# Moving the start of the large SBUF pools to multiples of 2048 bytes in a two-layer pool and SSD trunk

## The chip, the cores and the metric

The kernel runs on one core of one Trainium2 chip. The metric is the time of one execution on the device in microseconds (us); less is better. One further execution was profiled, and all rows below come from that one.

## The reference, cut to what matters

Two layers of the same form run one after the other on 256 tokens of 2048 channels, all in float32:

```python
h = rms_norm(x, pre_norm_w[layer])
proj = jnp.einsum('bld,de->ble', h, w_in[layer])      # 2048 -> 9248 columns
y_pool = pool_mixer(pool_u, pool_mix_w[layer], pool_scale[layer]) * silu(pool_gate)
y_ssd = ssd_branch(ssd_z, ssd_xbc, ssd_dt, ...)       # conv, chunked scan, gated norm
mixed = concatenate([y_pool, y_ssd])                  # 4096 channels
out = jnp.einsum('ble,ed->bld', mixed, w_out[layer])
x = x + rms_norm(out, post_norm_w[layer])
```

`pool_mixer` takes a trailing mean over 2, 4, 8 or 16 tokens, subtracts the token itself, and multiplies each of four channel groups with a 512 x 512 matrix.

## The kernel before, in words

Each float32 value that goes into a large product is split into a rounded high part and a rest, both of type float32r: `hs` holds the normalised input, `ms` and `pm` the two halves of `mixed`, `pl` the pooled channels, each as [128 partitions, k, 512] where the first 256 of the 512 columns are the high parts of the 256 tokens and the other 256 the rests. The weights come through a stream of 1 MB pieces: the SP queue loads a piece into one of three `raw` buffers (L122), ScalarE rounds half a piece to `wh` (L138), VectorE subtracts to get `wl` (L139), with five `wh` and five `wl` buffers.

In the input projection, and in the pool's 512 x 512 product, the weights are stationary and the activations move. `mm_m` (L330) issues a pair of matmuls for each 128 x 128 block of weights: L334 moves all 512 columns past `wh`, L336 moves the 256 high columns past `wl`. There are 2304 such pairs with `hs` (16 of them from `mm_k`, L342 and L344) and 128 with `pl`. In the output projection `out_mm` (L734) holds a block of `ms` or `pm` stationary and moves 512 columns of weights past it, three matmuls at a time (L741 to L743), 1536 in all. Every one of these matmuls loads its own stationary block.

Between the pairs PE gets the small products of the SSD branch, in plain float32: transposes (L288, L503), dt columns (L677), scores (L491), the scan's products (L537, L542), sums over channels (L325, L562). They are emitted by generators (`ssd`, `dt_chain`) that advance by one step at each `step_bg()` of `chunk`, so that their place among the large matmuls is set by the order of the program. Priorities (`P_SPLIT`, `P_EVAC`, `P_DT`) order the work on the other engines.

Where a tile lies in SBUF is set by the order in which the pools are opened and by the sizes in them. Each pool starts where the one opened ahead of it ends, and the first starts at byte 16512 of each partition. Before the change the order is `const`, `big`, `wts`, `work`. `const` takes 5120 bytes, so `big` starts at byte 21632, which is 1152 past a multiple of 2048. All tiles of `big` (`hs` and `pm` in one place, `ms`, `s16`) and of `wts` (`raw`, `wh`, `wl`) are multiples of 2048 bytes long, so all of them start at 1152 past a multiple of 2048. A [128, 512] float32 slice is 2048 bytes in each partition, a [128, 128] block of weights 512. In `work` lie the 4352-byte `t4` tiles, the 2048-byte `t2`, the 1024-byte `t1`, small tiles, and two buffers of 8192 bytes with the tag `t8`, which hold in turn the dt weights, `BC` (the scan's B and C), the broadcast decay, `pl` and the post-norm weights `pwb`. The `t8` buffers start at bytes 202432 and 210624, 1728 past a multiple of 2048.

The lines that the change and the prediction touch are the pools (L47 to L50), `t8` (L58), the constants (L205 to L233), `pl` (L704), `pwb` (L723) and the matmuls named above.

Of the kernel before, what the change touches and what calls it, by code (L numbers as in the profile page):

```python
# [8 lines left out]
F32 = mybir.dt.float32  # L9
F32R = mybir.dt.float32r  # L10
# [4 lines left out]
P = 128  # L15
D_MODEL = 2048
SEQ = 256
DEPTH = 2
NK = D_MODEL // P
NT = SEQ // P  # L20
CW = 512
# [9 lines left out]
NG = 4  # L31
# [10 lines left out]
def hybrid_kernel(ctx: ExitStack, tc, x, pre_norm_w, w_in, pool_mix_w, pool_scale, conv_w, conv_b,  # L42
# [1 line left out]
    nc = tc.nc  # L44
    PSUM = bass.MemoryType.PSUM

    const = ctx.enter_context(tc.tile_pool(name="const", bufs=1))  # L47
    big = ctx.enter_context(tc.tile_pool(name="big", bufs=1))
    wts = ctx.enter_context(tc.tile_pool(name="wts", bufs=1))
    work = ctx.enter_context(tc.tile_pool(name="work", bufs=1))  # L50
    dram = ctx.enter_context(tc.tile_pool(name="dram", bufs=1, space=bass.MemoryType.DRAM))
    ps_main = ctx.enter_context(tc.tile_pool(name="ps_main", bufs=4, space=PSUM))
    ps_aux = ctx.enter_context(tc.tile_pool(name="ps_aux", bufs=4, space=PSUM))
# [2 lines left out]
        return big.tile([P, 4, NT, CW], F32, name="s16", tag="s16", bufs=1)  # L56

    def t8():  # L58
        return work.tile([P, 8, SEQ], F32, name="t8", tag="t8", bufs=2)

    def t4():
        return work.tile([P, 4, PAD + SEQ], F32, name="t4", tag="t4", bufs=6)
# [116 lines left out]
    def drain_bg():  # L179
        while bg:  # L180
            step_bg()
# [23 lines left out]
    pre_rows = const.tile([DEPTH * NK, P], F32, name="pre_rows")  # L205
    load_pieces(x_in, emit_raw)

    ident = const.tile([P, P], F32, name="ident")
    make_identity(nc, ident)
    ones = const.tile([P, P], F32, name="ones")  # L210
    nc.vector.memset(ones, 1.0)
    upper = const.tile([P, P], F32, name="upper")
    nc.gpsimd.affine_select(out=upper, in_=ones, compare_op=ALU.is_ge, fill=0.0, base=0,
                            pattern=[[1, P]], channel_multiplier=-1)
    after = const.tile([P, P], F32, name="after")
# [3 lines left out]
    nc.vector.memset(eps, EPS)  # L219
    table = const.tile([P, 1], F32, name="table")  # L220
    nc.scalar.activation(out=table, in_=eps, func=AF.Copy)
    fac = const.tile([P, NG, 16], F32, name="fac")
    nc.gpsimd.memset(fac, 1.0)
    for g, w in enumerate(WINDOWS):
        for t in range(w - 1):
# [4 lines left out]
        nc.sync.dma_start(out=raw, in_=w_in[l, :, O_DT:O_DT + NH].rearrange("(k p) c -> p k c", p=P))  # L230
        return raw

    pre_cols = const.tile([P, DEPTH * NK], F32, name="pre_cols")  # L233
    def keep_busy(dst, n, after=None):
        with behind(after):
            for _ in range(n):
                ins = nc.tensor.matmul(dst[:, 0:P], ident, ident, start=True, stop=True, skip_group_check=True)  # L237
        return ins
# [108 lines left out]
    def chunk(mov, nk, pre_unit=None, mid_unit=None, by_k=False):  # L347
        acc = [main() for _ in range(4)]
        nq = nk // 4

        def mid(q, i):
            if mid_unit is not None:
                mid_unit(q, i)
            if q < nq - 1:
                step_bg()

        for q in range(nq):
            if pre_unit is not None:
                pre_unit(q)
            if q == 0 and by_k:  # L360
                hf = [next_half(), next_half()]
                for h in range(2):
                    for kk in range(2):
                        for m in range(4):
                            mm_k(acc, m, hf[h], mov, 2 * h, kk)
                        if h == 1:
                            mid(q, kk)
            elif 0 < q < nq - 1:
                for h in range(2):
                    hf = next_half()  # L370
                    for m in range(4):
                        mm_m(acc, m, hf, mov, 4 * q + 2 * h, False, False)
                    mid(q, h)
            else:
                last = q == nq - 1
                hf = [next_half(), next_half(not last)]
                for m in range(4):
                    for h in range(2):
                        mm_m(acc, m, hf[h], mov, 4 * q + 2 * h, q == 0 and h == 0, last and h == 1)
                    if m % 2 == 1:  # L380
                        mid(q, m // 2)
        return acc
# [8 lines left out]
    def evac(acc, dest, rb, sums=None):  # L391
        for m in range(4):
            t = halves_sum(acc[m]) if sums is None else sums[m]
            nc.gpsimd.tensor_tensor(out=dest[:, m], in0=t, in1=rb, op=ALU.mult)  # L394

    def conv_silu(l, acc, rb, ct0, dst, sums=None):
        pad = t4()
        nc.gpsimd.memset(pad[:, :, 0:KCONV - 1], 0.0)
        evac(acc, pad[:, :, KCONV - 1:KCONV - 1 + SEQ], rb, sums)
        cw = prm[l]["convw"]  # L400
        cb = prm[l]["convb"]
        for m in range(4):
            ct = ct0 + m
            nc.vector.tensor_scalar(out=dst[:, m], in0=pad[:, m, 3:3 + SEQ], scalar1=cw[:, 3, ct:ct + 1],
                                    scalar2=cb[:, ct:ct + 1], op0=ALU.mult, op1=ALU.add)
            for j in (2, 1, 0):
                nc.vector.scalar_tensor_tensor(out=dst[:, m], in0=pad[:, m, j:j + SEQ],  # L407
                                               scalar=cw[:, j, ct:ct + 1], in1=dst[:, m],
                                               op0=ALU.mult, op1=ALU.add)
        nc.scalar.activation(out=dst, in_=dst, func=AF.Silu)  # L410
# [212 lines left out]
    for l in range(DEPTH):  # L623
# [61 lines left out]
        for g in range(NG):  # L685
            acc = chunk(hs, NK)
            if g == 0:
                drain_bg()
            xs = t4()[:, :, 0:SEQ]
            conv_silu(l, acc, rb, 4 * g, xs)  # L690
            res = {}
            bg.append(ssd(l, g, st, xs, BC, res, ms))

            acc = chunk(hs, NK)
            zs = t4()[:, :, 0:SEQ]
            evac(acc, zs, rb)
            nc.scalar.activation(out=zs, in_=zs, func=AF.Silu)
            res["zs"] = zs

            acc = chunk(hs, NK)  # L700
            u = t4()
            nc.gpsimd.memset(u[:, :, 0:PAD], 0.0)
            evac(acc, u[:, :, PAD:PAD + SEQ], rb)
            pl = work.tile([P, 4, CW], F32R, name="pl", tag="t8", bufs=2)  # L704
            pool_window(g, u, pl)

            acc = chunk(hs, NK)
            gs = t4()[:, :, 0:SEQ]
            evac(acc, gs, rb)
            nc.scalar.activation(out=gs, in_=gs, func=AF.Silu)  # L710

            acc = chunk(pl, 4)
            for m in range(4):
                t = halves_sum(acc[m])
                nc.vector.scalar_tensor_tensor(out=pr[:, 4 * g + m], in0=t,
                                               scalar=prm[l]["scale"][:, 4 * g + m:4 * g + m + 1],
                                               in1=gs[:, m], op0=ALU.mult, op1=ALU.mult)
            if g == 1 and l + 1 < DEPTH:
                bg.append(load_params(l + 1))
        drain_bg()  # L720

        load_pieces(x_in if l == 0 else x_mid)
        pwb = work.tile([P, D_MODEL], F32, name="pwb", tag="t8", bufs=2)  # L723
        nc.gpsimd.dma_start(out=pwb, in_=post_norm_w[l].partition_broadcast(P))
        pm = big.tile([P, NK, CW], F32R, name="pm", tag="hs", bufs=1)
        for g in range(NG):
# [129 lines left out]
```

## Time and profile before

| | us |
|---|---|
| median of three runs | 1278.93 |
| lowest and highest | 1278.65, 1279.44 |
| the profiled execution | 1280.09 |
| its span, first to last instruction | 1278.3 |
| PE busy in the span | 1265.3 |

PE is TensorE's matmuls, PEld its weight loads, DVE VectorE, ACT ScalarE, POOL GpSimd, SP the queue that issues most DMAs. Matmuls are pipelined, so that the duration of one is longer than the distance to the next: what a matmul costs in a dense stream is read from the distance of the starts.

### The profile page before, as it was taken

What the parts mean: (1) busy time and instruction counts of PE and PEld (TensorE: products, weight loads), DVE (VectorE), ACT (ScalarE), POOL (GpSimd) and SP (SyncE); (2) the same over time, 40 slices, a digit from 0 to 9 for tenths busy, and PEclk for the clock granted to TensorE, in tenths of its full rate; (3) what the DMA queues carried; (4) which work ended last, traced back from release to release, by engine and by line L of the source; (5) the groups of instructions that cost most, each with busy time, mean ns of one, the idle gap of its engine ahead of it and who ended that gap; (6) DMA issues with size and microseconds to landing.
All of it is one profiled execution on the core that took longest, in us unless ns stands there. A gap on an engine that the chain in (4) does not pass through costs nothing.

```text
span 1278.3 us, 17942 instructions
## 1 busy us (share of the span) xinstructions
PE 1265.3 (99%) x7010; PEld 1084.8 (85%) x7010; DVE 919.0 (72%) x1299; ACT 707.0 (55%) x891; POOL 193.0 (15%) x244
## 2 busy tenths in 40 slices
PE   8999999999999999999999999999999999999997
PEld 7788888888888888888878888888888888888886
DVE  5898778868778794444478988778788788844454
ACT  6656556566566574344374566566565665644442
POOL 0111212212213220000002122122112122200000
PEclk9999999999999999999999999999999999999999
DMA  8555455464464676555564654555654654865552
GB/s 278 201 198 198 165 199 203 152 237 165 165 242 154 207 269 204 190 188 194 188 214 162 220 177 168 203 193 168 227 198 139 223 195 168 296 198 197 192 187 83
DMA packets 126973, 249.49 MB, mean 195 GB/s; under 512 B 9272, under 2 KB 10120, under 8 KB 125608
## 3 DMA queue, kind: packets, MB, share of 16 engines
q1 hardware_dynamic: 124792, 237.25, 54.8%
q0 software_dynamic: 1504, 10.55, 2.2%
q8 instruction: 55, 0.90, 0.3%
q10 hardware_dynamic: 592, 0.54, 0.1%
q14 instruction: 30, 0.25, 0.1%
HBM read 244.06 MB, written 4.26 MB: 194 GB/s over the span
## 4 chain that ended last, share of the span: by engine, by line
PE 99%; DVE 0%; DMA 0%; ACT 0%; issue 0%; ACTq 0%
PE acc L334 44%; PE acc L336 22%; PE acc L743 9%; PE acc L741 9%; PE acc L742 9%; PE aux L537 1%; PE aux L677 1%; PE aux L542 1%; PE aux L288 1%; PE aux L503 1%; DMA pre_rows<-in_pre_norm_w_dram 0%; PE acc L342 0%; DVE t L759 0%; PE aux L562 0%; PE aux L491 0%; PE aux L237 0%
## 5 line engine op out<-in xcount | busy, mean ns | idle before, releaser
L334 PE MATMUL acc<-hs,wh 128*128 128x512 f32 x2288 | 805.4, 396 | 1.0 <-DVE hs L298 1.0
L139 DVE TENSOR_TENSOR wl<-raw,wh 128x1024 fp32r<-128x1024 f32 x431 | 535.5, 1251 | 249.9 <-ACT wh L138 249.9
L138 ACT ACTIVATE wh<-raw 128x1024 fp32r<-128x1024 f32 x431 | 451.2, 1058 | 408.1 <-PE acc L334 215.8
L336 PE MATMUL acc<-hs,wl 128*128 128x256 f32 x2288 | 639.5, 280 | 0.0
L334 PEld LDWEIGHTS acc<-hs,wh 128*128 128x128 f32 x2288 | 428.5, 187 | 101.1 <-issue 1.7
L336 PEld LDWEIGHTS acc<-hs,wl 128*128 128x128 f32 x2288 | 431.8, 189 | 1.1 <-DVE wl L139 0.2
L394 POOL TENSOR_TENSOR t<-t,rb 128x256 f32<-128x256 f32 x144 | 139.5, 977 | 414.9 <-DVE t L388 375.1
L387 ACT COPY t<-acc 128x256 f32<-128x256 f32 x176 | 63.0, 366 | 69.2 <-PE acc L336 69.0
L741 PE MATMUL acc<-wh,pm 128*128 128x512 f32 x256 | 99.7, 389 | 0.0
L742 PE MATMUL acc<-wl,ms 128*128 128x512 f32 x256 | 99.6, 389 | 0.0
L743 PE MATMUL acc<-wh,ms 128*128 128x512 f32 x256 | 99.6, 389 | 0.0
L743 PE MATMUL acc<-wh,pm 128*128 128x512 f32 x256 | 99.6, 389 | 0.0
L742 PE MATMUL acc<-wl,pm 128*128 128x512 f32 x256 | 99.6, 389 | 0.0
L741 PE MATMUL acc<-wh,ms 128*128 128x512 f32 x256 | 99.6, 389 | 0.0
L388 DVE TENSOR_TENSOR t<-acc,t 128x256 f32<-128x256 f32 x176 | 71.3, 416 | 14.4 <-ACT t L387 13.6
L407 DVE SCALAR_TENSOR_TENSOR t<-t,cols,t 128x256 f32<-128x256 f32 x144 | 71.2, 525 | 0.1
L743 PEld LDWEIGHTS acc<-wh,ms 128*128 128x128 f32 x256 | 48.1, 188 | 10.0
L742 PEld LDWEIGHTS acc<-wl,pm 128*128 128x128 f32 x256 | 48.1, 188 | 10.0
L743 PEld LDWEIGHTS acc<-wh,pm 128*128 128x128 f32 x256 | 48.1, 188 | 10.0
L741 PEld LDWEIGHTS acc<-wh,ms 128*128 128x128 f32 x256 | 48.1, 188 | 9.9
L742 PEld LDWEIGHTS acc<-wl,ms 128*128 128x128 f32 x256 | 48.1, 188 | 9.9
L741 PEld LDWEIGHTS acc<-wh,pm 128*128 128x128 f32 x256 | 48.1, 188 | 9.9
(155 smaller groups left out, 841.8 us busy)
## 6 DMA issues: line engine op xcount, KB each, us to landing
raw<-in_w_in_dram SPq DMA_DIRECT2D x143, 1024.0 KB, 4.9
raw<-in_w_out_dram SPq DMA_DIRECT2D x64, 1024.0 KB, 5.1
t<-acs POOLq DMA_DIRECT2D x8, 1024.0 KB, 5.1
raw<-in_pool_mix_w_dram SPq DMA_DIRECT2D x8, 1024.0 KB, 5.1
t<-in_x_dram SPq DMA_DIRECT2D x7, 512.0 KB, 8.9
pwb<-in_post_norm_w_dram POOLq DMA_DIRECT2D x2, 1024.0 KB, 6.5
x_mid<-t SPq DMA_DIRECT2D x8, 256.0 KB, 2.4
t<-x_mid SPq DMA_DIRECT2D x4, 512.0 KB, 7.9
```

What stands on the lines that cost most here:

```text
L138: hi = nc.scalar.activation(out=wh, in_=r, func=AF.Copy)
L139: lo = nc.vector.tensor_tensor(out=wl, in0=r, in1=wh.bitcast(F32), op=ALU.subtract)
L288: ins = nc.tensor.transpose(out=pts[k4 % 2][:, o + T * P:o + (T + 1) * P], in_=xp[c][:, T, k4 * P:(k4 + 1) * P], identity=ident)
L334: nc.tensor.matmul(acc[m], wh[:, kk, cs], mov[:, k0 + kk, :], start=first and kk == 0, stop=False, skip_group_check=True)
L336: stream["mm"] = nc.tensor.matmul(acc[m][:, 0:SEQ], wl[:, kk, cs], mov[:, k0 + kk, 0:SEQ], start=False, stop=last and kk == 1, skip_group_ ...
L387: nc.scalar.copy(out=t[0:n], in_=acc[0:n, SEQ:CW])
L388: nc.vector.tensor_tensor(out=t[0:n], in0=acc[0:n, 0:SEQ], in1=t[0:n], op=ALU.add)
L394: nc.gpsimd.tensor_tensor(out=dest[:, m], in0=t, in1=rb, op=ALU.mult)
L407: nc.vector.scalar_tensor_tensor(out=dst[:, m], in0=pad[:, m, j:j + SEQ], scalar=cw[:, j, ct:ct + 1], in1=dst[:, m], op0=ALU.mult, op1=ALU ...
L741: nc.tensor.matmul(oacc[T], ah, wh[:, kk], start=first and kk == 0, stop=False)
L742: nc.tensor.matmul(oacc[T], ah, wl[:, kk], start=False, stop=False)
L743: nc.tensor.matmul(oacc[T], al, wh[:, kk], start=False, stop=last and kk == 1)
```

## The change

A new pool `first` is opened ahead of the others and takes `ident`, `ones`, `upper` (512 bytes each), `fac` (256) and `pre_cols` (128), 1920 bytes together. With the 16512 bytes in front of it that makes 18432, nine times 2048, and there `big` starts. The rest of the constants stays in `const`, which is now opened last. The two `t8` buffers, and with them `pl` and `pwb`, move from `work` to `wts`. So `hs`, `pm`, `ms`, `s16`, `raw`, `wh`, `wl` and the `t8` buffers start at multiples of 2048, and `work` starts at one. No instruction is added, removed or given another shape.

```diff
-    const = ctx.enter_context(tc.tile_pool(name="const", bufs=1))
+    first = ctx.enter_context(tc.tile_pool(name="first", bufs=1))
     big = ctx.enter_context(tc.tile_pool(name="big", bufs=1))
     wts = ctx.enter_context(tc.tile_pool(name="wts", bufs=1))
     work = ctx.enter_context(tc.tile_pool(name="work", bufs=1))
+    const = ctx.enter_context(tc.tile_pool(name="const", bufs=1))
...
     def t8():
-        return work.tile([P, 8, SEQ], F32, name="t8", tag="t8", bufs=2)
+        return wts.tile([P, 8, SEQ], F32, name="t8", tag="t8", bufs=2)
...
-    ident = const.tile([P, P], F32, name="ident")
+    ident = first.tile([P, P], F32, name="ident")
...
-    ones = const.tile([P, P], F32, name="ones")
+    ones = first.tile([P, P], F32, name="ones")
...
-    upper = const.tile([P, P], F32, name="upper")
+    upper = first.tile([P, P], F32, name="upper")
...
-    fac = const.tile([P, NG, 16], F32, name="fac")
+    fac = first.tile([P, NG, 16], F32, name="fac")
...
-    pre_cols = const.tile([P, DEPTH * NK], F32, name="pre_cols")
+    pre_cols = first.tile([P, DEPTH * NK], F32, name="pre_cols")
...
-            pl = work.tile([P, 4, CW], F32R, name="pl", tag="t8", bufs=2)
+            pl = wts.tile([P, 4, CW], F32R, name="pl", tag="t8", bufs=2)
...
-        pwb = work.tile([P, D_MODEL], F32, name="pwb", tag="t8", bufs=2)
+        pwb = wts.tile([P, D_MODEL], F32, name="pwb", tag="t8", bufs=2)
```

## Rows read from the trace of the kernel before

**Rows 1.** The page, parts 1 and 2: busy time, and clock in 40 slices

```profile
PE 1265.3 (99%) x7010; PEld 1084.8 (85%) x7010; DVE 919.0 (72%) x1299; ACT 707.0 (55%) x891; POOL 193.0 (15%) x244
PEclk9999999999999999999999999999999999999999
```

**Rows 2.** The page, part 4: the chain that ended last, by engine

```profile
PE 99%; DVE 0%; DMA 0%; ACT 0%; issue 0%; ACTq 0%
```

**Rows 3.** Waits of the whole span: waiter, releaser, us in total, times, longest

```profile
ACT wh L138 <- DMA raw<-in_w_out_dram: 2.6, 1, 2.6
PE acc L334 <- DVE hs L298: 1.0, 1, 1.0
```

**Rows 4.** Busy time by stage: us, then each engine's busy time, clock, DMA

```profile
0.00:32.00 32.00, 27.63 (x156) 24.36 (x157) 17.60 (x32) 20.61 (x43) 2.33 (x38) 1.00 0.87 277
630.00:660.00 30.00, 28.97 (x158) 24.09 (x156) 21.12 (x33) 16.75 (x31) 0.11 (x1) 1.00 0.64 201
1268.00:1278.30 10.30, 2.73 (x13) 1.92 (x11) 4.80 (x8) 1.70 (x4) 1.69 (x1) 0.77 0.54 204
```

**Rows 5.** Timeline of PE, output projection of layer 0: start, duration, instruction

```profile
500.49 0.39 PE L741 MATMUL acc<-wh,pm 128*128 128x512 f32 x1
...
505.93 0.39 PE L741 MATMUL acc<-wh,pm 128*128 128x512 f32 x1
```

**Rows 6.** Timeline of PE, 157.5 to 200 us: `hs`, then `pl`, then `hs`

```profile
157.54 0.39 PE L334 MATMUL acc<-hs,wh 128*128 128x512 f32 x1
...
159.27 0.40 PE L334 MATMUL acc<-pl,wh 128*128 128x512 f32 x1
159.50 0.28 PE L336 MATMUL acc<-pl,wl 128*128 128x256 f32 x1
...
164.93 0.39 PE L334 MATMUL acc<-hs,wh 128*128 128x512 f32 x1
165.16 0.28 PE L336 MATMUL acc<-hs,wl 128*128 128x256 f32 x1
165.27 0.40 PE L334 MATMUL acc<-hs,wh 128*128 128x512 f32 x1
...
199.94 0.39 PE L334 MATMUL acc<-hs,wh 128*128 128x512 f32 x1
```

**Rows 7.** Timeline of PE behind L542, 124 to 142 us

```profile
124.24 1.16 PE L542 MATMUL aux<-scs,t 128*128 128x128 f32 x8
...
125.94 0.40 PE L334 MATMUL acc<-hs,wh 128*128 128x512 f32 x1
...
141.84 0.40 PE L334 MATMUL acc<-hs,wh 128*128 128x512 f32 x1
```

**Rows 8.** The chain in order of time: start, us, plain float32 matmuls

```profile
101.46 0.43 PE aux L491 x2
104.89 0.87 PE aux L503 x8
...
201.15 0.43 PE aux L491 x2
```

**Rows 9.** Groups by line and form: count, busy us, mean ns, idle before

```profile
L139 DVE TENSOR_TENSOR wl<-raw,wh 128x1024 fp32r<-128x1024 f32 x431 | 535.5, 1251 | 249.9 <-ACT wh L138 249.9
L759 DVE SCALAR_TENSOR_TENSOR t<-s,r,t 128x512 f32<-128x512 f32 x15 | 11.0, 766 | 0.2
L574 DVE TENSOR_TENSOR pm<-s,pm 128x1024 fp32r<-128x1024 f32 x8 | 10.0, 1270 | 0.0
L574 DVE TENSOR_TENSOR pl<-t,pl 128x1024 fp32r<-128x1024 f32 x8 | 9.6, 1194 | 0.0
```

## Prediction, made before the change was run

> **What bounds the kernel now.** I read the page's busy time first: PE is busy for 1265.3 of 1278.3 us, at the full clock in all 40 slices [rows 1]. Next the chain that ended last: 99% of it is PE [rows 2]. Then the waits: the longest of a weight split for a landing is one of 2.6 us, and PE itself waited 1.0 us for its input [rows 3]. The stages show where PE is idle at all: 32.00 - 27.63 = 4.4 us at the start, 1.0 us between the layers, 7.6 us at the end [rows 4], together the 13.0 us that busy time and span differ by. So the change can pay in one way only: a matmul must follow the one before it sooner. The other engines' durations can touch no more than those 13 us.
>
> Busy time doesn't show the distance of matmuls, so I went to the starts. In the output projection 24 matmuls of 512 columns start between 500.49 and 505.93 us: 5.44 / 24 = 226.7 ns each [rows 5]. In the input projection 100 pairs of 512 + 256 columns start between 165.27 and 199.94 us: 34.67 / 100 = 346.7 ns a pair [rows 6]. With a fixed price a for each matmul and b for a column, a + 512b = 226.7 and 2a + 768b = 346.7 give b = 0.417 ns and a = 13.3 ns. That b is one column a cycle at 2.4 GHz, the level granted, so the columns leave nothing to gain. The a is the question: 2 x 2432 pairs' matmuls and 1536 others are 6400 matmuls, and 6400 x 13.3 = 85 us, the most that any layout could free. The dense stream makes up 2432 x 0.3467 + 1536 x 0.2267 = 1191 us of the span.
>
> **The change part by part.** No instruction and no wait is added, removed or moved in a queue; SP and POOL issue the same DMAs. Addresses alone change, and they change in three groups.
>
> *hs, pm, ms, s16, raw, wh, wl, and nearly all of work.* `big` and the rest of `wts` move by 18432 - 21632 = -3200 bytes; t4, t2 and the tiles near them by -3200 + 16384, because the t8 pair is now in front of them; those behind t8's old place by -3200 again. As 16384 is a multiple of 2048, all these keep their distances to each other modulo 2048. What changes is the absolute place: 1152 past a multiple of 2048 becomes 0, and for the matmuls that means that a moving run of 2048 or 1024 bytes no longer crosses a multiple of 2048, as every one of the 6400 now does. The trace of before has no large matmul that doesn't cross, so the price of crossing has to be bounded. Lower bound 0: a block of weights starts at 128, 640, 1152 or 1664 past, by the column block m, and only the last crosses; the pair keeps its 346.7 ns through stretches that run over all four [rows 6]. The same for moving runs, but in slow plain float32: C in L491 starts at 1728 for an even group and 704 for an odd one; the first crosses, the second doesn't, and two of them take 0.43 us either way [rows 8]. Upper bound: the whole a. A new block of weights need not cost 13.3 ns as such: the eight transposes of L503 load one each and take 0.87 us, 109 ns for 128 columns; L491 takes 215 ns for 256. The same sum gives 0.83 ns a column and about 2.5 ns fixed [rows 8]. So up to 13.3 - 2.5 = 10.8 ns of each large matmul is special to float32r at one column a cycle. It may be the weight load, which has no slack to hide in at that rate, or the layout. I take 0, because the only rows that compare crossing with not crossing show no difference, and keep 6400 x 10.8 = 69 us as the other end.
>
> *pl.* Here the trace has a comparison. The stream runs without a break from hs to pl and back to hs. The five hs pairs ahead take 1.73 us, 346 ns each; the 16 pairs with pl from 159.27 to 164.93 us take 5.66 / 16 = 353.8 ns; behind them it is 346.7 again [rows 6]. Same instructions and weight buffers; what differs is where the moving operand starts: pl at 1728, 576 from hs modulo 2048, so 64 past a multiple of 128, where hs and all weights lie at such multiples. The change puts pl at 0, the same distance from the weights as hs. I take the whole difference: 8 products x 16 pairs x 6.8 ns = 0.9 us less; the bounds are 0 and 0.9. The Trainium skill ("SBUF — State Buffer", Specifications and Door 1) knows of lines of 16 bytes that cost when crossed; 1152 and 1728 are both multiples of 16, so by that page pl and hs should run alike and this part would bring 0. The rows differ by 7 ns a pair, so here the measurement goes ahead of the page.
>
> *The beat behind an insertion.* The slower beat isn't pl's alone. Behind the L542 matmuls hs runs 45 pairs in 141.84 - 125.94 = 15.90 us, 353.3 ns each [rows 7], though 20 us later the same tiles run at 346.7. The stream takes up a beat when it starts again and keeps it until the next insertion. This comes in the same place in each of the eight groups (46 pairs in seven, 22 in the eighth), and with shorter runs about 590 of the 2304 pairs are in it: 590 x 6.7 = 3.9 us. The beat seems to hang on the last small matmuls ahead, and some of their operands do shift against hs: ident and ones by 128 modulo 512, t8 by 64. L542's own (scs and t2) don't. So I leave this at 0, with bounds: 3.9 us less if all restarts come out fast; more if the two restarts that are fast now (behind L503, 46 pairs a group; behind L562, some 150) come out slow: 8 x 196 x 6.7 = 10.5 us.
>
> *Other engines.* VectorE's subtraction of the same shape means 1194 ns on pl, 1251 on weights and 1270 on pm [rows 9]; were that spread all layout, it would move the 431 splits by 431 x 0.057 = 25 us, but VectorE is busy for 919 of 1278 us [rows 1], and PE covers it. Without that cover, in the start, the turn and the end, some ten such instructions lie in the chain; 10 x 0.057 = 0.6 us either way. I take 0. Landings of the 1 MB pieces are covered by the buffers ahead, the one wait of 2.6 us aside [rows 3].
>
> The sum for the profiled execution: 1280.1 - 0.9 = 1279.2. It ran 1.2 us over the median of the three runs (its span 1278.3 and 1.8 us around it), so against the median it is 1278.9 - 0.9 = 1278.0 us.
>
> **The rivals.** (1) The fixed price is the layout's: a moving operand that crosses a multiple of 2048, or starts off one, costs each large matmul up to 10.8 ns. Then all 6400 gain, 69 us: 1278.9 - 69 - 0.9 = 1209; if a is freed in full, 1193; half of it, 1244. For it: plain float32 shows only 2.5 ns, pl shows that the start of a moving operand can matter, and each large matmul crosses exactly once, whatever its length. Against it: stationary blocks that cross cost nothing, L491 shows nothing, and hs and pl, 576 bytes apart, differ by 7 ns in 27. The Trainium skill ("TensorE: Matmul & The Clock Gate", Back-to-back issue gap) gives N/2.4 + 2.5 ns for warm matmuls, which is the same 2.5 ns; it doesn't say what keeps float32r from it. (2) The restarts come out fast: pl and the 590 pairs all gain, 1278.9 - 0.9 - 3.9 = 1274.1. (3) Slower: ident and ones now lie 128 off the grid of the others, and the stream restarts in the slow beat behind L503 and L562. That gives 1278.0 + 10.5 = 1288.5, and it decides against the 0.9 us of pl as soon as some 520 more pairs go slow (0.9 + 2.6 us, at 6.7 ns each). For it: the beat changes from one kind of insertion to the next. Against it: the operands of L542, behind which it is slow today, aren't the ones that shift. (4) The change doesn't do what it says. By the sizes, 16512 + 1920 = 18432 = 9 x 2048 and every tile in front of pl is a multiple of 2048 long, so I give that no chance of its own; it would leave 1278.9, inside my forecast.
>
> **How the numbers follow.** A measurement of this kernel can tell about 0.2% (2.6 us) from no change; the three runs lie within 0.06%. My forecast, 1278.0 with 1276.4 to 1281.4 for small shifts of beat, gets 0.54. Rival 1 gets 0.19, rival 2 0.12, rival 3 in full or part 0.15. Faster is 0.19 + 0.12 = 0.31, same 0.54, slower 0.15. The range holds the forecast, rival 2 and rival 3 (0.81): from 1272, which is rival 2 with 0.6 us at the ends and 1.5 us of what lies about the profile, to 1289. Rival 1 is left out; for it one would have to go down to 1193.
>
> **What would show it.** If I am right, the starts in the output projection stay 226.7 ns apart, hs pairs 346.7, and pl pairs come down from 353.8 to 346.7. Rival 1 shows as 216 ns in the output projection and 325 ns a pair. Rivals 2 and 3 show only behind insertions, in whether the 46 pairs behind L542 and L503 take 353.3 or 346.7 ns each. The forecast is wrong if the distance of the output projection's matmuls changes at all, since nothing else there can move.

## Result and profile after the change

The changed kernel is slower: 1287.29 us (median of five executions, 1287.13 to 1287.39) against 1279.14 for the kernel before, measured beside it (1278.65 to 1280.08). The ratio is 1.0063, with a 95% interval of 1.0048 to 1.0077. The profiled execution took 1287.14 us with a span of 1285.4; against the profiled execution of before (1280.09, span 1278.3) that is 7.1 us. The other 1.1 us between the medians is mostly that the profiled execution of before lay 0.95 us over its median.

All line numbers of the changed kernel are one higher (L334 is L335, L503 is L504, L542 is L543, L562 is L563). The order of the instructions is the same on every engine. The page of after, busy time, clock and the chain by engine, answers to [rows 1, 2]:

```profile
PE 1272.6 (99%) x7010; PEld 1085.6 (84%) x7010; DVE 916.0 (71%) x1299; ACT 706.8 (55%) x891; POOL 199.0 (15%) x244
PEclk9999999999999999999999999999999999999999
PE 99%; DVE 0%; DMA 0%; ACT 0%; issue 0%; ACTq 0%
```

PE is busy 7.3 us longer with the same 7010 matmuls, and it is 99% of the chain as before. The granted clock shows the same digit, 9 for nine tenths or more, in all 40 slices, and its mean over the span is 0.998 in both. So the 7.1 us are PE's: its idle time in the span is 12.8 us, against 13.0 before. In the groups by line, first before and then after (count, busy us and mean ns of one), the difference stands nearly whole in one line:

```profile
L334 PE MATMUL acc<-hs,wh 128*128 128x512 f32 x2288 | 805.4, 396 | 1.0 <-DVE hs L298 1.0
L336 PE MATMUL acc<-hs,wl 128*128 128x256 f32 x2288 | 639.5, 280 | 0.0
```

```profile
L335 PE MATMUL acc<-hs,wh 128*128 128x512 f32 x2288 | 812.8, 400 | 1.0 <-DVE hs L299 1.0
L337 PE MATMUL acc<-hs,wl 128*128 128x256 f32 x2288 | 640.6, 280 | 0.0
```

The output projection, which was to be the first test, is unchanged. In the timeline of PE (start, duration, instruction) 24 matmuls take 505.96 - 500.52 = 5.44 us, 226.7 ns each, as in [rows 5]:

```profile
500.52 0.39 PE L742 MATMUL acc<-wh,pm 128*128 128x512 f32 x1
...
505.96 0.39 PE L742 MATMUL acc<-wh,pm 128*128 128x512 f32 x1
```

The input projection isn't. The same timeline over one group of heads, behind the transposes of L504, behind L538 and L543, and behind L563:

```profile
105.20 1.04 PE L504 MATMUL aux<-ident,t 128*128 128x128 f32 x8
...
106.77 0.40 PE L335 MATMUL acc<-hs,wh 128*128 128x512 f32 x1
...
122.67 0.40 PE L335 MATMUL acc<-hs,wh 128*128 128x512 f32 x1
...
126.36 0.40 PE L335 MATMUL acc<-hs,wh 128*128 128x512 f32 x1
...
142.30 0.40 PE L335 MATMUL acc<-hs,wh 128*128 128x512 f32 x1
142.66 0.59 PE L563 MATMUL aux<-t,ones 128*128 128x256 f32 x2
143.44 0.40 PE L335 MATMUL acc<-hs,wh 128*128 128x512 f32 x1
...
160.05 0.40 PE L335 MATMUL acc<-pl,wh 128*128 128x512 f32 x1
...
165.70 0.40 PE L335 MATMUL acc<-hs,wh 128*128 128x512 f32 x1
...
202.10 0.40 PE L335 MATMUL acc<-hs,wh 128*128 128x512 f32 x1
```

Behind L504 45 pairs take 122.67 - 106.77 = 15.90 us, 353.3 ns each. Behind L543 46 pairs take 142.30 - 126.36 = 15.94 us, 346.5 ns, where the same stretch of before took 353.3 [rows 7]. From 165.70 on 103 pairs take 36.40 us, 353.4 ns, where before had 346.7 [rows 6]. The 16 pairs with `pl` take 5.65 us, 353.1 ns: hardly less than the 353.8 read before [rows 6].

So the stretches between two insertions still run in one of two beats, 346.7 or 353.3 ns from pair to pair, and what changed is which. (The few at the start of a layer that hold waits have no clear beat.) For the count below, a pair's cost is the distance from the start of its long matmul to the start of the next one, averaged over the stretch from one insertion to the next (waits left out); a stretch over 350.5 ns is called slow. 2295 pairs lie in such stretches. With another rule for what is a wait the totals move by up to some 15 pairs.

| slow pairs behind | pairs | before | after |
|---|---|---|---|
| L503, transposes (`ident`) | 344 | 0 | 344 |
| L542, second scan products (`scs`, `t2`) | 368 | 322 | 46 |
| L562, sums over channels (`ones`): `hs` | 994 | 0 | 994 |
| the same stretch: `pl` | 126 | 126 | 126 |
| all other insertions | 463 | 258 | 287 |
| all | 2295 | 706 | 1797 |

That is 1091 more slow pairs, and 1091 x 6.67 ns (353.33 - 346.67) = 7.3 us: the busy time of PE to the tenth.

### The profile page after: what moved, and what is told of

It reads as the page before. It is cut to its first block, busy times and chain, and to the rows that moved or that the text cites. A ratio compares the mean times of both kernels' runs of the same rounds, so it can differ in the third digit from the quotient of the medians.

```text
span 1285.4 us, 17942 instructions
## 1 busy us (share of the span) xinstructions
PE 1272.6 (99%) x7010; PEld 1085.6 (84%) x7010; DVE 916.0 (71%) x1299; ACT 706.8 (55%) x891; POOL 199.0 (15%) x244
## 4 chain that ended last, share of the span: by engine, by line
PE 99%; DVE 0%; DMA 0%; ACT 0%; issue 0%; ACTq 0%
PE acc L335 44%; PE acc L337 22%; PE acc L742 9%; PE acc L744 9%; PE acc L743 9%; PE aux L538 1%; PE aux L678 1%; PE aux L543 1%; PE aux L289 1%; PE aux L504 1%; DMA pre_rows<-in_pre_norm_w_dram 0%; PE acc L343 0%; DVE t L760 0%; PE aux L492 0%; PE aux L563 0%; PE aux L238 0%
## 5 line engine op out<-in xcount | busy, mean ns | idle before, releaser
L335 PE MATMUL acc<-hs,wh 128*128 128x512 f32 x2288 | 812.8, 400 | 1.0 <-DVE hs L299 1.0
L140 DVE TENSOR_TENSOR wl<-raw,wh 128x1024 fp32r<-128x1024 f32 x431 | 532.0, 1243 | 254.7 <-ACT wh L139 254.4
L335 PEld LDWEIGHTS acc<-hs,wh 128*128 128x128 f32 x2288 | 429.5, 188 | 107.3 <-issue 1.7
```

The costliest lines, as they stand in the source:

```text
L140: lo = nc.vector.tensor_tensor(out=wl, in0=r, in1=wh.bitcast(F32), op=ALU.subtract)
L335: nc.tensor.matmul(acc[m], wh[:, kk, cs], mov[:, k0 + kk, :], start=first and kk == 0, stop=False, skip_group_check=True)
```

## The experiments

In the expectations, theory I says that the place of `ident` and `ones` against `hs` and the weights sets the beat (Ia: each behind the small matmuls that read it), II that the absolute place of the large tiles does it, III that the moved t8 pair does it, IV that the moment at which the stream resumes sets it, and that the addresses act through that alone. Places below are bytes past that of `hs`, modulo 2048. Before has `ident` at 1536, `ones` at 0, t8 at 576; after has 128, 640 and 0. The columns L503, L542, L562 count slow pairs behind these insertions (of 344, 368 and 994), `pl` of 126. Each row is one execution, the profiled one. In the text the insertions keep the names that they have in before or after; in the timelines lines that a run adds shift them (L567 in e5 is L562).

| kernel | `ident` | `ones` | t8 | L503 | L542 | L562 | `pl` | all | span, us |
|---|---|---|---|---|---|---|---|---|---|
| before | 1536 | 0 | 576 | 0 | 322 | 0 | 126 | 706 | 1278.3 |
| after | 128 | 640 | 0 | 344 | 46 | 994 | 126 | 1797 | 1285.4 |
| e1 | 1664 | 128 | 576 | 18 | 322 | 300 | 62 | 864 | 1280.5 |
| e2 | 1536 | 0 | 0 | 0 | 322 | 0 | 0 | 687 | 1278.9 |
| e3 | 1536 | 0 | 0 | 0 | 322 | 0 | 30 | 706 | 1278.1 |
| e4 | 1536 | 0 | 576 | 0 | 368 | 0 | 46 | 536 | 1278.1 |
| e5 | 128 | 0 | 0 | 160 | 230 | 0 | 30 | 783 | 1278.8 |
| e6 | 1536 | 640 | 0 | 0 | 322 | 994 | 126 | 1721 | 1284.6 |
| e7 | 128 | 640 | 0 | 298 | 92 | 947 | 111 | 1622 | 1285.0 |
| e8 | 1536 | 0 | 0 | 0 | 368 | 0 | 15 | 723 | 1279.0 |
| e11 | 640 | 128 | 0 | 344 | 46 | 994 | 126 | 1684 | 1284.1 |
| e12 | 128 | 640 | 0 | 344 | 46 | 994 | 126 | 1884 | 1286.2 |

In before, e1, e2 and e8 `hs` itself lies at 1152, in e12 at 128, in the others at 0. Without e7, which has matmuls added, a straight line through the eleven spans gives 1274.5 us plus 6.0 ns for each slow pair, and no kernel is over 0.9 us off it. To within that, the count of slow pairs explains the spans, whatever else was moved. Executions of one kernel differ too: the ten of e1 took 1279.62 to 1282.27 us, and the profiled one is the slowest of them; the four of e11 took 1285.89 to 1288.20, and the profiled one is the fastest. Two microseconds are some 300 pairs, so a difference of that size between two rows need not come from the layout.

**e1, the constants alone.** The kernel before, with `pre_cols` (128 bytes) laid ahead of `ident` and `ones`, so that both are shifted by 128. The small constants between them and the old place of `pre_cols` (`upper`, `after` and three that PE doesn't read) shift with them; the large tiles and t8 stay.

```diff
+    pre_cols = const.tile([P, DEPTH * NK], F32, name="pre_cols")
     ident = const.tile([P, P], F32, name="ident")
...
-    pre_cols = const.tile([P, DEPTH * NK], F32, name="pre_cols")
```

> The kernel before with one edit: pre_cols (128 bytes) is laid in front of ident and ones, so that these two start 128 bytes past the 512-byte grid of hs, wh and wl, as they do after the change; the big tiles and t8 stay where they were. Theory I (the beat at which the pair stream restarts is set by where the small matmuls' own operands ident and ones lie against the grid of the large tiles): the restarts behind L503 and L562 come out slow (353.3 ns a pair instead of 346.7), those behind L542 fast, and the time goes to about 1287 us. Theory II (the absolute place of the large tiles sets it): nothing moves, 1279 us. Theory III (t8's place sets it): nothing moves, 1279 us.

Measured: 1280.38 us, ratio 1.0005 (0.9995 to 1.0015). The beat did change, behind L562 in 300 of 994 pairs, but mostly it didn't: a shift of 128 against the weights isn't enough by itself to make a kernel as slow as after. And half of the 300 lie in a group in which PE had waited 0.18 us for VectorE in the middle of the pairs behind L503:

```profile
106.32 0.40 PE L334 MATMUL acc<-hs,wh 128*128 128x512 f32 x1
...
115.34 0.39 PE L334 MATMUL acc<-hs,wh 128*128 128x512 f32 x1
...
116.03 0.50 PE L334 MATMUL acc<-hs,wh 128*128 128x512 f32 x1 [0.18 <-DVE t L388]
...
116.48 0.40 PE L334 MATMUL acc<-hs,wh 128*128 128x512 f32 x1
...
122.84 0.40 PE L334 MATMUL acc<-hs,wh 128*128 128x512 f32 x1
```

The 26 pairs up to the wait take 346.9 ns each and the 18 from 116.48 on 353.3, with no small matmul between them. So a wait alone can change the beat. Away from the start of a layer, eight more stretches, in e1, e3, e4, e5 and e8, went from fast to slow on the way; in each a load of `wl` weights had just waited 12 to 39 ns for VectorE's split. Six such waits, of 19 to 37 ns, left the beat as it was.

**e2, t8 alone.** The kernel before with the two `t8` buffers, `pl` and `pwb` among them, in `wts`.

```diff
     def t8():
-        return work.tile([P, 8, SEQ], F32, name="t8", tag="t8", bufs=2)
+        return wts.tile([P, 8, SEQ], F32, name="t8", tag="t8", bufs=2)
...
```

> The kernel before with the t8 buffers alone moved to wts, behind wl, so that pl and the other t8 tiles start on the grid of hs, wh and wl (1152 past a multiple of 2048); ident and ones stay at their place, and so do the big tiles. Theories I and II: the restarts stay as they were, the pl pairs alone come down from 353.5 to 346.7 ns, and the time is 0.9 us less, 1278.1 us. Theory III: the restarts behind L491 and L537, whose operands are in t8, change beat; the time goes towards 1287 us.

Measured: 1279.86 us, ratio 1.0001 (0.9992 to 1.0011). The `pl` step of the prediction came true: all eight stretches run at 346.7 ns. Here 15 pairs take 165.66 - 160.46 = 5.20 us:

```profile
160.46 0.39 PE L334 MATMUL acc<-pl,wh 128*128 128x512 f32 x1
...
165.66 0.39 PE L334 MATMUL acc<-pl,wh 128*128 128x512 f32 x1
```

But the 118 pairs behind L426, fast before, were slow in this execution, and 126 against 118 leaves next to nothing. Theory III falls for the 8 us.

**e3 and e4, the large tiles with and without t8.** e3 is the kernel after with `ident` and `ones` where they had been against `hs`; e4 is e3 with the t8 pair back in `work`. To get the places, the constants are created in another order and in two more pools, and one small tile is set to zero.

```diff
+    at_ones = ctx.enter_context(tc.tile_pool(name="at_ones", bufs=1))
+    rest = ctx.enter_context(tc.tile_pool(name="rest", bufs=1))
+    upper = first.tile([P, P], F32, name="upper")
+    fac = first.tile([P, NG, 16], F32, name="fac")
+    pre_cols = first.tile([P, DEPTH * NK], F32, name="pre_cols")
+    pre_rows = first.tile([DEPTH * NK, P], F32, name="pre_rows")
+    ident = first.tile([P, P], F32, name="ident")
+    ones = at_ones.tile([P, P], F32, name="ones")
...
```

> The kernel after the change, with ident put at 1536 and ones at 0 past a multiple of 2048, which is the distance to hs that they had before (pre_rows takes ident's room in the first pool, ones goes behind work, with 32 bytes of filler). The big tiles and t8 are at multiples of 2048 as after the change. Theory I: the slow restarts are gone, the pl pairs run at 346.7 ns too, 1278 us. Theory II: as after the change, 1287 us. Theory III: as after the change, 1287 us.

> As the run before it, with the t8 buffers back in work, 576 past a multiple of 2048, so that everything but upper, after and the small constants keeps its distance to hs modulo 2048 that it had before, and only the absolute place moves to multiples of 2048. Theory I: the beats of the kernel before, pl pairs at 353.5 ns, 1279 us. Theory II: 1287 us. Theory III: 1279 us.

Measured: 1280.15 us, 1.0004 (0.9995 to 1.0013), and 1279.10 us, 0.9996 (0.9987 to 1.0006). In both, `hs`, `ms`, `pm` and the weights lie at multiples of 2048, in e3 the t8 pair too, and the loss is gone: no slow pair behind L503 or L562. Theory II falls. Nor is there a gain: the alignment by itself brought nothing that can be measured, either way.

**e5 and e6, one constant at a time.** The kernel after, in e5 with `ones` back at 0 and `ident` left at 128, in e6 with `ident` back at 1536 and `ones` left at 640. Other small tiles make room for them: of those that PE reads, `pre_rows` and `after` move in e5, `upper` in e6.

In e5:

```diff
+    ident = first.tile([P, P], F32, name="ident")
+    pre_rows = first.tile([DEPTH * NK, P], F32, name="pre_rows")
+    upper = first.tile([P, P], F32, name="upper")
+    fac = first.tile([P, NG, 16], F32, name="fac")
+    pre_cols = first.tile([P, DEPTH * NK], F32, name="pre_cols")
+    ones = at_ones.tile([P, P], F32, name="ones")
...
```

In e6:

```diff
+    upper = first.tile([P, P], F32, name="upper")
+    ones = first.tile([P, P], F32, name="ones")
+    fac = first.tile([P, NG, 16], F32, name="fac")
+    pre_cols = first.tile([P, DEPTH * NK], F32, name="pre_cols")
+    ident = first.tile([P, P], F32, name="ident")
...
```

> The kernel after the change with ones alone put back to its old distance from hs (0 past a multiple of 2048, behind work; pre_rows takes its room in the first pool); ident stays at 128, upper, fac and pre_cols where the change put them. Theory Ia (each restart takes its beat from the operand of the small matmuls just ahead of it): behind L563 the stream is fast again (346.7 ns, some 150 pairs in each of eight groups, 8.0 us), behind L504 it stays slow: 1279.3 us. Theory Ib (ident is what counts, and the beat is handed on from one insertion to the next): 1287 us. Theory II (ident and ones don't act, it was upper or another small tile that the earlier layout moved along): 1287 us with all beats as after the change.

> The kernel after the change with ident alone put back to its old distance from hs (1536 past a multiple of 2048); ones stays at 640, upper moves by 1024 to 128, pre_rows stays where the change put it. Theory Ia: behind L504 the stream is fast (46 pairs in eight groups, 2.5 us), behind L563 it stays slow: 1284.8 us. Theory Ib: all restarts as in the kernel before, 1279 us. Theory II: 1287 us, or 1279 us if upper's move by 1024 is what acts.

Measured: e5 1280.58 us, 1.0002 (0.9993 to 1.0011); e6 1286.32 us, 1.0049 (1.0034 to 1.0064). The timeline of PE in e5, behind the sums over channels:

```profile
142.82 0.59 PE L567 MATMUL aux<-t,ones 128*128 128x256 f32 x2
...
159.89 0.39 PE L339 MATMUL acc<-pl,wh 128*128 128x512 f32 x1
...
165.44 0.39 PE L339 MATMUL acc<-hs,wh 128*128 128x512 f32 x1
...
201.15 0.39 PE L339 MATMUL acc<-hs,wh 128*128 128x512 f32 x1
```

103 pairs take 201.15 - 165.44 = 35.71 us, 346.7 ns, and the 16 with `pl` ahead of them 5.55 us, 346.9 ns. Moving one tile of 512 bytes, which only small matmuls read (with `pre_rows` and the constants behind it making room), takes the whole loss back. In e6 the beat behind the transposes, behind L543 and behind L563:

```profile
105.52 0.39 PE L335 MATMUL acc<-hs,wh 128*128 128x512 f32 x1
...
121.11 0.40 PE L335 MATMUL acc<-hs,wh 128*128 128x512 f32 x1
...
125.16 0.40 PE L335 MATMUL acc<-hs,wh 128*128 128x512 f32 x1
...
141.06 0.40 PE L335 MATMUL acc<-hs,wh 128*128 128x512 f32 x1
...
164.45 0.40 PE L335 MATMUL acc<-hs,wh 128*128 128x512 f32 x1
...
200.85 0.40 PE L335 MATMUL acc<-hs,wh 128*128 128x512 f32 x1
```

The three stretches: 45 pairs in 15.59 us (346 ns), 45 in 15.90 (353.3), 103 in 36.40 (353.4). `ident` back at its place makes all 344 pairs behind the transposes fast, but the stretch behind L543 turned round with them: 276 pairs went slow there. So e6 is only 1 us under after. Ia holds for `ones` in these two runs. For `ident` it holds in one direction: at 1536 no restart behind the transposes is slow, at 128 all are in after, but only 160 of 344 in e5, where `ones` is back.

This turning round is no single case: in the eleven kernels of the table that issue L537 ahead of L542, eight groups each, the beat behind them is the opposite of the one that ran into them, 88 times of 88. Before goes from fast to slow, after from slow to fast, and in one of the eight groups, where the parameter transposes of L268 lie between L503 and L542, it follows the beat behind L268 (slow there in before and e6, and fast behind L542; fast in after, and slow).

**e7 and e8, the restart.** e7 is after with one more transpose of `ident` behind L563; e8 is e2 with the scan's second products (L542) issued ahead of the first (L537).

In e7:

```diff
         nc.tensor.matmul(pn[:, 0:SEQ], ones, sq[:, 0], start=True, stop=True)
+        nc.tensor.transpose(out=pn[:, SEQ:SEQ + P], in_=ident, identity=ident)
```

In e8, put ahead of the loop that holds L537 and taken away behind it:

```diff
+        ob = aux()
+        for j in range(4):
+            nc.tensor.matmul(ob[:, j * P:(j + 1) * P], xde[:, j * P:(j + 1) * P], scs[:, 2],
+                             start=True, stop=True, skip_group_check=True)
```

> The kernel after the change with one transpose of ident added behind the sum over channels (L563), eight in all, into columns that nobody reads; no address is changed. By the 109 ns that one such transpose takes, it adds 0.9 us of work. Theory I, in the form that the place of ones fixes the beat behind L563: the stream stays slow there, 1288.2 us. Theory IV (what sets the beat is the moment in which the stream restarts, to a few cycles, and the addresses act through that alone): the restart behind L563 can change to the fast beat with addresses unchanged, which brings 8.0 us less the 0.9: 1280.2 us.

> The kernel before with t8 on the grid of hs, and the scan's second products (four matmuls) issued ahead of its first (sixteen), so that the stream restarts behind others than before; the work is the same. Theory I: the beat behind the pair of products changes to the fast one, since their operands are others, in 46 pairs of eight groups: 1279.2 - 2.5 = 1276.7 us. Theory IV: it may change or not, and the runs of 46 pairs tell; if it stays slow, 1279 us.

Measured: e7 1287.75 us, 1.0063 (1.0046 to 1.0080); e8 1280.58 us, 1.0004 (0.9995 to 1.0014). In e7 another instruction stands last ahead of the stream, one that reads `ident`, and 947 of 994 pairs stay slow. In e8 the other small products stand last, and all 368 pairs behind them are slow. In seven groups the fast beat ran in, so these can't tell; in the eighth the slow one did (22 pairs from 314.95 to 322.72 us, 353.2 ns each), and it stays slow (45 pairs from 326.76 to 342.67 us, 353.6):

```profile
314.95 0.39 PE L334 MATMUL acc<-hs,wh 128*128 128x512 f32 x1
...
322.72 0.40 PE L334 MATMUL acc<-hs,wh 128*128 128x512 f32 x1
...
326.76 0.40 PE L334 MATMUL acc<-hs,wh 128*128 128x512 f32 x1
...
342.67 0.40 PE L334 MATMUL acc<-hs,wh 128*128 128x512 f32 x1
```

So 109 ns more ahead of the stream moved few restarts. That speaks against IV in its plain form, but it is one delay only, and the waits shown under e1 did change the beat with nothing moved and no small matmul ahead. And the turning round goes with the order of L537 and L542, since in e8 it is missing in that one group. e7 also has one group of another kind (behind L504 fast, behind L543 slow, behind the transpose fast), where all addresses are those of the others; so the place of the constants is not the only thing that counts (more on this under e11 and e12).

**e9 and e10, the beat itself.** Two long matmuls, then two short ones, in the kernel before and in the kernel after.

```diff
         for kk in range(2):
             nc.tensor.matmul(acc[m], wh[:, kk, cs], mov[:, k0 + kk, :],
                              start=first and kk == 0, stop=False, skip_group_check=True)
+        for kk in range(2):
             stream["mm"] = nc.tensor.matmul(acc[m][:, 0:SEQ], wl[:, kk, cs], mov[:, k0 + kk, 0:SEQ],
```

> The kernel before with one change of order: two blocks of weights at a time are issued as 512, 512, 256, 256 columns instead of 512, 256, 512, 256. Same matmuls, same addresses. Theory: the two beats of a pair (346.7 and 353.3 ns) are two ways in which the weight loads fall between a long and a short matmul; with two of a kind side by side there is no such choice, every four matmuls take 693.3 ns (two pairs of 346.7), and the 706 slow pairs give back 706 x 6.67 ns = 4.7 us: 1274 to 1275. If the beat is kept by the restart whatever the order, some 700 pairs stay at 353.3 ns and the time stays at 1279. If the load of a weight block doesn't fit beneath 256 columns twice in a row, four matmuls take more than 706 ns and the time rises: 10 ns in each of 1216 groups would make 1291.

> The kernel after with the same change of order (512, 512, 256, 256 columns). Theory: without the choice between two beats the place of ident and ones costs nothing, so it runs like the kernel before in this order, within 1 us, and some 8 to 12 us under the changed kernel (1274 to 1279). If the beat is kept whatever the order, it stays some 8 us above the kernel before in this order.

Measured: e9 1279.01 us, 0.9995 (0.9986 to 1.0004), span 1277.2; e10 1278.98 us, 0.9993 (0.9984 to 1.0003), span 1277.7. The dependence on the layout is gone: after in this order is as fast as before, 7.7 us of span under itself in the old order. In e10's timeline (two matmuls of a kind in a row stand as one line):

```profile
165.62 0.62 PE L335 MATMUL acc<-hs,wh 128*128 128x512 f32 x2
...
200.45 0.63 PE L335 MATMUL acc<-hs,wh 128*128 128x512 f32 x2
```

50 groups of four matmuls take 34.83 us, 696.6 ns each, and over the whole span the mean is 696.7 in e9 and 696.8 in e10. There is one beat now, but it isn't the fast one: two fast pairs would be 693.3 ns, two slow ones 706.7. So the expected 4.7 us didn't come, and no version here beats the kernel before beyond what can be measured.

**e11 and e12, which property of the address.** e11 is after with `ident` and `ones` in each other's place. e12 is after with 128 unused bytes in front, so that every tile lies 128 higher and no large one starts at a multiple of 2048.

In e11, then in e12:

```diff
+    ones = first.tile([P, P], F32, name="ones")
     ident = first.tile([P, P], F32, name="ident")
-    ones = first.tile([P, P], F32, name="ones")
```

```diff
+    pad = first.tile([P, 32], F32, name="pad")
     ident = first.tile([P, P], F32, name="ident")
```

> The kernel after with ident and ones in each other's place: ones 128 and ident 640 past a multiple of 2048, where after has 128 and 640 the other way round. Both keep their distance of 128 modulo 512 to hs and the weights. If that distance alone sets the beat, nothing changes: the stream behind L563 (994 pairs) and behind L504 (344 pairs) stays slow, 1287. If the place modulo more than 512 counts, one of the two goes fast: behind L563 fast would give 994 x 6.67 = 6.6 us back (some 1280 to 1281, with what L543's restarts do), behind L504 alone about 1 to 2 us (1285 to 1286).

> The kernel after with 128 unused bytes in front of ident: every tile lies 128 bytes higher, so that ident is 256, ones 768 and hs, the weights and the t8 buffers 128 past a multiple of 2048. All distances between tiles are those of after; what changes is the absolute place, and that nothing starts at a multiple of 2048 any more. If the distances set the beat, it stays as in after: behind L563 (L564 here) 994 slow pairs and behind L504 344, 1287. If the absolute place acts, the beat behind the sums over channels becomes that of e1_ident_ones_off, whose ident, ones and hs lie at the same places modulo 512 (256, 256, 128): some 300 of 994 slow and 18 behind the transposes, 1280 to 1281.

Measured: e11 1287.62 us, 1.0063 (1.0046 to 1.0080); e12 1287.79 us, 1.0055 (1.0039 to 1.0072). Neither changes a restart behind L504, L543 or L563. In e12 the stretch of 103 pairs takes 202.26 - 165.86 = 36.40 us, 353.4 ns, as in after:

```profile
165.86 0.40 PE L336 MATMUL acc<-hs,wh 128*128 128x512 f32 x1
...
202.26 0.40 PE L336 MATMUL acc<-hs,wh 128*128 128x512 f32 x1
```

So a shift of all tiles by 128 changes nothing as long as the distances between them stay, and neither does exchanging two places with the same distance modulo 512. Modulo 512 e1 has that distance too, and mostly kept the fast beat. The traces show what sets it apart: how the stream runs into the sums over channels. In the slow beat every third pair takes 361 ns and the two others 349 or 350. In e1 the sums (L562) cut this cycle with two pairs behind the 361 ns one in six groups, and the stream comes out fast; in one group they cut it with one pair behind, and it comes out slow. (Into the eighth, the one with the wait, the fast beat ran; it comes out slow too.) One of the six, then the one:

```profile
242.47 0.40 PE L334 MATMUL acc<-hs,wh 128*128 128x512 f32 x1
...
242.83 0.40 PE L334 MATMUL acc<-hs,wh 128*128 128x512 f32 x1
...
243.18 0.40 PE L334 MATMUL acc<-hs,wh 128*128 128x512 f32 x1
...
243.53 0.59 PE L562 MATMUL aux<-t,ones 128*128 128x256 f32 x2
```

```profile
342.94 0.40 PE L334 MATMUL acc<-hs,wh 128*128 128x512 f32 x1
...
343.30 0.40 PE L334 MATMUL acc<-hs,wh 128*128 128x512 f32 x1
...
343.65 0.59 PE L562 MATMUL aux<-t,ones 128*128 128x256 f32 x2
```

Counted over all twelve kernels of the table, eight restarts behind the sums in each, this fits without an exception. Where `ones` lies at 0 modulo 512 (before, e2, e3, e4, e5, e8), all 48 are fast, whatever ran in. Where it lies at 128 modulo 512 (after, e1, e6, e7, e11, e12), all 29 into which the fast beat ran are slow, and so are the 12 into which the slow beat ran with one pair behind the 361 ns one; the 7 with two pairs behind it, six in e1 and one in e7, are fast. So e1, e7 and e11 follow one rule: the place of `ones` and the point of the cycle at which the sums cut in decide together. This was read from the traces afterwards, and no run was made to test it; of distances modulo 512, only 0 and 128 occur. Behind the transposes the place of `ident` counts in the same way, all 48 restarts fast at 0 and 35 of 48 slow at 128, but no such sign was found for the 13 others.

## Why the prediction was wrong, step by step

**What bounds the kernel: right.** PE alone sets the time. (The digit 9 in the clock's slices says nine tenths or more, not full: in the last 10.3 us of before it was 0.77 [rows 4], but there PE is busy for 2.7 us only.) Busy time rose by 7.3 us and the span by 7.1. VectorE's weight split even became a little shorter, 1243 ns instead of 1251 [rows 9], without any effect on the end.

**Large tiles off and on the grid: right.** The 0 held. The output projection kept its 226.7 ns to the tenth, so the 69 us of rival 1 weren't there, and the fixed 13.3 ns of a float32r matmul isn't the price of crossing a multiple of 2048. By the Trainium skill's formula for a single warm matmul ("TensorE: Matmul & The Clock Gate", Back-to-back issue gap) 512 columns would take 512 / 2.4 + 2.5 = 215.8 ns, an estimate; the output projection stays 11 ns over it whether its operands cross a multiple of 2048 or not.

***pl*: right by itself, lost in the whole.** With t8 in `wts` and the constants left alone (e2), `pl` runs at 346.7 ns in all eight stretches. In before, e1 and e4, which keep t8 576 past `hs`, none of the 24 stretches does: they take 349.2 to 353.6. The Trainium skill's lines of 16 bytes ("SBUF — State Buffer", Specifications and Door 1) would make 0 and 576 alike, and these stretches show that they aren't. What the step left out is that `pl` also rides on the beat that its stretch took up at L562. That beat was fast before, so the offset was all that could be seen; in after it is slow, and `pl` stays at 353.1.

**The beat behind an insertion: the step that failed.** It was left at 0 with an upper bound of 10.5 us, though the mechanism had been seen and priced. It measured 7.3 us, 1091 more pairs in the slow beat. The reason given was that the operands of L542, "behind which it is slow today, aren't the ones that shift". That took one rule to hold for all insertions. The runs show two: behind L503 and L562 the place of the constant that the small matmuls read counts (e5, e6), together with the way in which the beat runs in (e1), while behind L537 and L542 the beat turns round whatever it was. So the slow beat behind L542 in [rows 7] was no evidence on the operands of L542 at all; it followed from the fast beat behind L503. The trace of before held the sign: in the one group with L268 between L503 and L542, the 22 slow pairs stand behind L268 (314.20 to 321.97 us, 353.2 ns each) and the 46 behind L542 are fast (325.66 to 341.61 us, 346.7 ns). The prediction had counted those 22 as L542's.

```profile
313.68 0.30 PE L268 MATMUL aux<-ident,rows 96*128 96x96 f32 x1
...
314.20 0.39 PE L334 MATMUL acc<-hs,wh 128*128 128x512 f32 x1
...
321.97 0.40 PE L334 MATMUL acc<-hs,wh 128*128 128x512 f32 x1
...
325.66 0.40 PE L334 MATMUL acc<-hs,wh 128*128 128x512 f32 x1
...
341.61 0.40 PE L334 MATMUL acc<-hs,wh 128*128 128x512 f32 x1
```

The sign that the prediction named for being wrong, another distance in the output projection, watched a stream without such insertions and didn't show; the `hs` pairs, named beside it, did.

**Rival 3: right in the place of the loss, in size 7.3 us instead of 10.5.** It put the loss down to `ident` and `ones` lying 128 off the grid of the others; the runs show that this counts (e6 against e3) but isn't enough (e1). It took 8 x 196 = 1568 pairs; 344 + 994 = 1338 were really newly slow behind L503 and L562, because it had counted the `pl` pairs, which were slow already, and full groups everywhere. These are 1338 x 6.67 = 8.9 us. The turning round at L542 gave 276 x 6.67 = 1.8 back, and the other insertions took 29 pairs, 0.2 us: 8.9 - 1.8 + 0.2 = 7.3. The time lies 1.2 us under the 1288.5 worked out for it. The forecast had 0.54 and this rival 0.15; with the reason against it gone, the rows gave no ground to rank the forecast so far above it.

**Rival 2: the other sign of the same thing.** It needed all restarts fast. The nearest kernel, e4, has 536 slow pairs instead of 706, and its 1279.10 us can't be told from before. By the line through the spans, no slow pair at all would be a span of 1274.5, an estimate; no kernel here came near.

**What stays open** is why. The runs show that the two beats belong to the alternation of long and short matmuls (e9, e10), that a beat is taken up at a restart and can change at a wait, and that behind the sums the place of `ones` and the beat that ran in decide together. They don't show which part of PE or of its reads from SBUF keeps it, nor whether the place of a constant acts otherwise than through the moment of the restart.

## What to carry to other kernels

Where PE is the bound and the clock is full, read the distance of matmul starts separately for every stretch between two insertions: a stream can run in more than one beat, and a layout change can exchange them by moving a small tile that the stream itself never reads. Laying large tiles at round addresses was worth nothing here, but putting the constants of the small matmuls elsewhere cost 0.6%, so a layout change should keep the distances of what it doesn't mean to move. An order that leaves the stream one beat (long, long, short, short) gives up 1.7 ns a pair against the best case and gave the same time in the two layouts tried (e9, e10).

## What the runs showed of the hardware that was not expected

- A stream of float32r matmuls of 512 and 256 columns in turn has two beats, 346.7 and 353.3 ns a pair, both at a granted clock of 1.00. All stretches of 103 pairs keep the one they took up at their start. Nine shorter ones went from fast to slow on the way, each at a wait: one of 0.18 us of PE (e1), the others of 12 to 39 ns of a weight load.
- The place of an operand of a small matmul ahead of the stream helps to decide which: with `ones` 640 bytes past the place of `hs` instead of 0, 994 pairs take the slow beat, and the span is 6.5 us longer (e6 against e3, 1284.6 against 1278.1). At a distance of 128 modulo 512 the beat that runs in counts as well: 41 restarts of 48 slow, 7 fast.
- A moving operand 576 bytes off the weights' place modulo 2048 runs at 349.2 to 353.6 ns a pair, even where the stretch ahead of it is fast (353.6 in before, 349.2 in e4); it was never seen at 346.7.
- The small products of L537 and L542 turn the beat round; behind them it was the opposite of the one ahead in 88 groups of 88.
